# Pairs of branch weights in one fetch, one summed block of squares per norm, and one activation part kept twice, in a hybrid decoder layer

## The chip, the cores and the metric

The kernel runs on one NeuronCore of a Trainium2 chip. The metric is the device time of one execution in microseconds; for a kernel the median of several executions is given. TensorE (PE) multiplies, VectorE (DVE), ScalarE (ACT) and GpSimd (POOL) work on elements, and SyncE (SP) issues most of the DMAs.

## The reference

One decoder layer for a single sequence of 256 tokens, model width 2048, all in float32:

```python
h = rms_norm(x, ln1)
proj = h @ w_in                      # gdn q|k|v, beta, decay, z, moba q|k|v, gate a, gate b
y_a = gated_deltanet(...) @ w_branch_a      # 8 heads of 128, chunks of 64
y_b = moba_attention(...) @ w_branch_b      # 8 heads of 128, 256 tokens are one block: causal attention
merged = sigmoid(gate_a) * y_a + sigmoid(gate_b) * y_b
x = x + merged @ w_out
h = rms_norm(x, ln2)
u = causal_dwconv(h @ w_up, ffn_conv, bias)  # width 3, 2 x 5632 columns
x = x + (silu(u_gate) * u_val) @ w_down
return rms_norm(x, final_norm)
```

`rms_norm(x, w)` is `x * rsqrt(mean(x * x) + 1e-6) * w`.

## The kernel before, in words

**Arithmetic.** Each large product is made of three products of rounded parts. A weight is split into a high part `wh` (its value rounded to the type that PE reads, fp32r) and a low part `wl` (the rest); an activation into `one(k, 0)` and `one(k, 1)` in the same way. `block` multiplies, for each block k of 128 input channels, `wh` by the high part, `wh` by the low part and `wl` by the high part, and adds all of it up in one PSUM tile. The channels of the output lie on the partitions and the 256 tokens on the free axis, so that a product has a 128x128 weight block and 256 moving columns. The norms' factor per token (`R1`, `R2`) is multiplied in after the product (`join`), so that PE needn't wait for it.

**Stages, in the order of the program.** The first gdn blocks, in which the inputs arrive; then gdn and z (three chunks and one, for four pairs of heads), moba q and k (eight chunks) with v (four chunks of another form), gate (16 chunks), the two branch projections, called br (8 times a chunk for branch a and one for branch b), wo (8 chunks), up (44 chunks) and down, with the final norm. A chunk is two output blocks of 128 channels. It has 96 main products where the input has 16 blocks (gdn, z, moba, gate, wo, up), and 48 in br, whose input has 8.

**Weights.** `fetch` lets SP copy a weight block into one of four `wraw` buffers of 128x2048 words. `load_w` then makes the parts in pieces of 1024 columns: ACT casts (`wh`, L121) and DVE subtracts (`wl`, L118). There are two `wh` and two `wl` tiles, which take turns, and one call of `load_w` takes one of each, whatever it puts in. In br a call brings 1024 columns, half a tile, and in the other stages 2048.

**Background.** The short steps of the delta rule and of attention are generators in a list `bg`; each time that the main products' estimated cost passes `EVERY`, `tick` advances them by a step. Their small products stand between main products in PE's queue until the gate stage is some chunks old.

**Where operands lie.** `Parts` holds both parts of an activation in one tile, for k = 0 to 15 the high part and then the low part, 256 words each. After the eighth k there is a gap of 64 words, and `TURN` (0 here) could move a low part into it. Weights start 24 words into their tile (`PLACE`, 8 for v).

**Kicks.** Before a chunk that `KICKS` names (gate 7, wo 1, up 1, 12, 23 and 34) three products with 128 moving columns are issued into a tile that nobody reads.

**Norms.** ACT squares, DVE and POOL add blocks of channels up, and `rstd` sums over the partitions with products by a tile of ones (float32, L99). For the first norm two blocks of 128x256 are left at that point, for the second four, which come as two pairs (`sqa`, and `sq` of the last chunk).

**The end.** For each of two halves of the tokens and four column blocks n, ACT squares the finished sum in PSUM (L836), and for n < 3 DVE multiplies it by the final norm's weights (L839). Then come a reduction (L840), a square root, a reciprocal (L842), and the scaling of the four blocks (L845 for n = 3, L847, L849) with their output DMAs.

The order on each engine is set by the framework's scheduler from its own simulation, and each engine works strictly along its list.

Of the kernel before, what the change touches and what calls it, by code (L numbers as in the profile page):

```python
# [11 lines left out]
F32 = mybir.dt.float32  # L12
# [17 lines left out]
PLACE = {"v": 8}  # L30
TURN = 0
KICKS = {"gate": (7,), "wo": (1,), "up": (1, 12, 23, 34)}
GROUP = 8
ATT_SCALE = 128 ** -0.5
# [49 lines left out]
def layer_kernel(ctx: ExitStack, tc: tile.TileContext, xT, pos, cst, csel, ceye, vec, convw, ffw, bdv,  # L84
# [68 lines left out]
    class Parts:  # L153


        def __init__(self, pool, kt, name, **kw):
            self.size = GROUP * 2 * T + 64
            self.flat = pool.tile([P, kt // GROUP * self.size], F32R, name=name, **kw)

        def at(self, k, a):  # L160
            return k // GROUP * self.size + (2 * (k % GROUP) + a) * T + TURN * (a and k % GROUP == GROUP - 1)

        def one(self, k, a):
            o = self.at(k, a)
            return self.flat[:, o:o + T]

        def two(self, k, a):
            o, step = self.at(k, a), self.at(k + 1, a) - self.at(k, a)
            if o + 2 * step <= self.flat.shape[1]:
                return self.flat[:, o:o + 2 * step].rearrange("p (b t) -> p b t", b=2)[:, :, :T]  # L170
            o -= step - T
            return self.flat[:, o:o + 2 * step].rearrange("p (b t) -> p b t", b=2)[:, :, step - T:]

# [14 lines left out]

    def block(ps, j, w, x, kt, k0=0, k1=None):
        wh, wl = (r3(t, P) for t in w)  # L190
        for k in range(k0, k1 or kt):
            for w_, a in ((wh, 0), (wh, 1), (wl, 0)):
                main_mm(ps[:, j], w_[:, k, :], x.one(k, a), j == k == a == 0 and w_ is wh,
                        k == kt - 1 and w_ is wl)

    def chunk(blocks, x, kt, name, raws=(None, None), piece=1024, steps=((0, 0, None), (1, 0, None)), c=None):
        ps = mmt("ps_" + name)
        ws = {}
        if c in KICKS.get(name, ()):
            ws[0] = load_w(blocks[0], kt * P, raw=raws[0], piece=piece, at=PLACE.get(name, 24))  # L200
            idle = sdt("kick")
            for _ in range(3):
                pe.matmul(idle[:, :P], ws[0][0][:, :P], x.one(0, 0)[:, :P], start=True, stop=True)
        for j, k0, k1 in steps:
            if j not in ws:
                ws[j] = load_w(blocks[j], kt * P, raw=raws[j], piece=piece, at=PLACE.get(name, 24))
            block(ps, j, ws[j], x, kt, k0, k1)
        return ps
# [23 lines left out]
    hp = hst.enter_context(tc.tile_pool(name="hp", bufs=1, side="right"))  # L232
    hc = Parts(hp, KD, "hc", tag="hc")
    front = ExitStack()
# [28 lines left out]
    for i in range(4):  # L263
        scaled(xs[:, 4 * i:4 * i + 4, :], ln1v, 4 * i, hc)
    raws = [fetch(w) for w in (w_gdn[2], w_gdn[3])]
    wbd = g.tile([P, KD, 16], F32, name="wbd")
# [29 lines left out]
    dve.tensor_tensor(sq[0], sq[0], sq[2], op=ALU.add)  # L296
    dve.tensor_tensor(sq[0][:, 0:2], sq[0][:, 0:2], sq[0][:, 2:4], op=ALU.add)


# [5 lines left out]
    mmg(s, [(wb2[:, k, :], hc.one(k, a)) for k in range(KD) for a in range(2)])  # L305
    R1 = rstd([sq[0][:, 0, :], sq[0][:, 1, :]], fk, "R1")
    R1b = both(R1)
# [420 lines left out]
    for c in range(8):  # L728
        bts = [yp.tile([P, 2, T], F32, name="bt", bufs=3) for _ in range(2)]
        join(bts[0], chunk(pair(w_ba, c), yc[0], H, "br"), gts[:, c])  # L730
        ps = chunk(pair(w_bb, c), yc[1], H, "br")
        if c < 7:
# [16 lines left out]
    sqa = b.tile([P, 2, T], F32, name="sqa", bufs=1)  # L749
    h2 = Parts(hp, KD, "h2", tag="hc")  # L750
    for c in range(8):
# [8 lines left out]
        if c == 0:  # L760
            act.activation(sqa, xc, AF.Square)
        else:
            sq = b.tile([P, 2, T], F32, name="sq2")
            act.activation(sq, xc, AF.Square)
            if c < 7:
                pool.tensor_tensor(sqa, sqa, sq, op=ALU.add)
    R2 = rstd([t[:, j, :] for t in (sqa, sq) for j in range(2)], bkeep, "R2")
    R2b = both(R2)
# [31 lines left out]
    def residual(i, n):  # L800
# [5 lines left out]
    wl = {}  # L806
    tail = hp.tile([P, KD // GROUP * (GROUP * 2 * T + 64)], F32R, name="tail", tag="hc")[:, :8192].rearrange(
        "p (t k n) -> p t k n", t=2, k=2)

# [19 lines left out]
    for i in range(2):  # L829
        sm = b.tile([P, 8], F32, name="sm")  # L830
        ots = []
        for n in range(4):
            for k in range(NF - LAST, NF):
                down(i, n, k, stop=(k == NF - 1))
            scr = b.tile([P, 512], F32, name="scr")
            act.activation(scr, pd[i][n], AF.Square, accum_out=sm[:, n:n + 1])  # L836
            ots.append(b.tile([P, 512], F32, name="ot_", bufs=5))
            if n < 3:
                dve.tensor_tensor(ots[n], pd[i][n], fw[:, n * 512:(n + 1) * 512], op=ALU.mult)  # L839
# [3 lines left out]
        for n in range(4):  # L843
            if n == 3:
                dve.scalar_tensor_tensor(ots[n], pd[i][n], sm[:, 6:7], fw[:, n * 512:], op0=ALU.mult, op1=ALU.mult)  # L845
# [71 lines left out]
```

## Time and profile before

| | |
|---|---|
| median of 3 executions | 1497.35 us (1497.07 to 1499.13) |
| the profiled execution | 1498.51 us, its span 1496.7 us |
| mean granted TensorE clock | 0.997 |
| PE busy | 1478.6 us, 11489 products |
| DVE, ACT, POOL busy | 967.8, 720.9, 121.2 us |
| read from HBM | 271.68 MB, 184 GB/s over the span |

The span runs from the first to the last instruction on the core; 1.8 us of the time lie around it. Products are pipelined: one of 256 columns is listed with 276 ns, but the next starts some 113 ns after it. "PE busy" therefore says that PE nearly always has a product under way, and not how fast they follow each other. The chain of waits gives the latter: its pieces join instructions that followed each other, with their count.

### The profile page before, as it was taken

What the parts mean: (1) busy time and instruction counts of PE and PEld (TensorE: products, weight loads), DVE (VectorE), ACT (ScalarE), POOL (GpSimd) and SP (SyncE); (2) the same over time, 40 slices, a digit from 0 to 9 for tenths busy, and PEclk for the clock granted to TensorE, in tenths of its full rate; (3) what the DMA queues carried; (4) which work ended last, traced back from release to release, by engine and by line L of the source; (5) the groups of instructions that cost most, each with busy time, mean ns of one, the idle gap of its engine ahead of it and who ended that gap; (6) DMA issues with size and microseconds to landing.
All of it is one profiled execution on the core that took longest, in us unless ns stands there. A gap on an engine that the chain in (4) does not pass through costs nothing.

```text
span 1496.7 us, 26967 instructions
## 1 busy us (share of the span) xinstructions
PE 1478.6 (99%) x11489; PEld 1418.4 (95%) x11489; DVE 967.8 (65%) x1373; ACT 720.9 (48%) x948; POOL 121.2 (8%) x133
## 2 busy tenths in 40 slices
PE   9999999999999999999999999999999999999998
PEld 8999999998999999999999999999999998888886
DVE  7978786896656545666666666666666665555554
ACT  5655363434474444345455544454554544444444
POOL 0001010141121000110100000000000000000000
PEclk9999999999999999999999999999999999999999
DMA  9545444444436554568555555555555555555552
GB/s 334 182 150 185 152 155 169 150 149 164 145 115 207 191 195 127 183 209 318 191 186 197 196 189 186 193 195 197 197 196 187 189 194 177 189 196 194 197 197 85
DMA packets 45658, 277.23 MB, mean 185 GB/s; under 512 B 5505, under 2 KB 6993, under 8 KB 15457
## 3 DMA queue, kind: packets, MB, share of 16 engines
q1 hardware_dynamic: 43712, 270.98, 52.7%
q0 software_dynamic: 960, 2.36, 0.5%
q10 hardware_dynamic: 864, 2.16, 0.4%
q8 instruction: 90, 1.47, 0.4%
q14 instruction: 32, 0.25, 0.0%
HBM read 271.68 MB, written 3.80 MB: 184 GB/s over the span
## 4 chain that ended last, share of the span: by engine, by line
PE 91%; DVE 4%; DMA 2%; ACT 1%; issue 1%; SPq 0%; DVEq 0%; ACTq 0%
PE ps_up L111 32%; PE pd L99 16%; PE ps_gate L111 11%; PE ps_gdn L111 8%; PE ps_wo L111 5%; PE ps_br L111 5%; PE ps_moba L111 4%; PE ps_v L111 3%; PE ps_z L111 3%; DVE wl L118 2%; DMA wraw<-in_w_gdn 1%; ACT wh L121 1%; DMA x<-in_xT 1%; PE g L99 1%; PE py L558 1%
## 5 line engine op out<-in xcount | busy, mean ns | idle before, releaser
L118 DVE TENSOR_TENSOR wl<-wraw,wh 128x1024 fp32r<-128x1024 f32 (+1 forms) x500 | 607.1, 1248 | 214.6 <-ACT wh L121 214.3
L121 ACT CAST wh<-wraw 128x1024 fp32r<-128x1024 f32 (+1 forms) x500 | 497.7, 1040 | 466.2 <-PE ps_up L111 162.7
L111 PE MATMUL ps_up<-h,wh 128*128 128x256 f32 x2816 | 479.7, 276 | 0.0
L111 PEld LDWEIGHTS ps_up<-h,wh 128*128 128x128 f32 x2816 | 424.2, 188 | 0.1
L111 PE MATMUL ps_up<-h,wl 128*128 128x256 f32 x1408 | 388.6, 276 | 0.0
L111 PEld LDWEIGHTS ps_up<-h,wl 128*128 128x128 f32 x1408 | 264.3, 188 | 0.0
L111 PE MATMUL ps_gate<-hc,wh 128*128 128x256 f32 x1024 | 176.8, 278 | 0.0
L111 PEld LDWEIGHTS ps_gate<-hc,wh 128*128 128x128 f32 x1024 | 154.6, 188 | 0.0
L111 PE MATMUL ps_gate<-hc,wl 128*128 128x256 f32 x512 | 141.9, 277 | 0.4 <-DVE wl L118 0.4
L99 PE MATMUL pd<-wl,ah 128*128 128x512 f32 x336 | 130.8, 389 | 0.0
L99 PE MATMUL pd<-wh,al 128*128 128x512 f32 x336 | 130.8, 389 | 0.0
L111 PE MATMUL ps_gdn<-hc,wh 128*128 128x256 f32 x704 | 126.7, 283 | 0.0
L111 PEld LDWEIGHTS ps_gdn<-hc,wh 128*128 128x128 f32 x704 | 108.9, 191 | 0.9 <-ACT wh L121 0.3
L111 PE MATMUL ps_gdn<-hc,wl 128*128 128x256 f32 x352 | 99.8, 284 | 0.8 <-DVE wl L118 0.8
L111 PEld LDWEIGHTS ps_gate<-hc,wl 128*128 128x128 f32 x512 | 96.2, 188 | 0.6 <-DVE wl L118 0.6
L111 PE MATMUL ps_moba<-hc,wh 128*128 128x256 f32 x512 | 93.1, 283 | 0.0
L99 PE MATMUL pd<-wh,ah 128*128 128x512 f32 x336 | 92.8, 391 | 0.0
L212 DVE TENSOR_TENSOR unf<-ps_up,R 128x512 f32<-128x512 f32 x44 | 30.4, 691 | 90.1 <-PE ps_up L111 90.1
L111 PE MATMUL ps_wo<-mc,wh 128*128 128x256 f32 x512 | 87.3, 276 | 0.0
L111 PEld LDWEIGHTS ps_moba<-hc,wh 128*128 128x128 f32 x512 | 78.6, 189 | 0.2
L111 PEld LDWEIGHTS ps_wo<-mc,wh 128*128 128x128 f32 x512 | 77.2, 188 | 0.0
L99 PEld LDWEIGHTS pd<-wh,al 128*128 128x128 f32 x336 | 63.1, 188 | 13.3
(426 smaller groups left out, 1966.5 us busy)
## 6 DMA issues: line engine op xcount, KB each, us to landing
wraw<-in_w_up SPq DMA_DIRECT2D x88, 1024.0 KB, 4.9
wraw<-in_w_dn SPq DMA_DIRECT2D x44, 1024.0 KB, 4.8
wraw<-in_w_gate SPq DMA_DIRECT2D x32, 1024.0 KB, 4.9
wraw<-in_w_gdn SPq DMA_DIRECT2D x30, 1024.0 KB, 5.0
wraw<-in_w_moba SPq DMA_DIRECT2D x16, 1024.0 KB, 4.9
wraw<-in_w_o SPq DMA_DIRECT2D x16, 1024.0 KB, 4.9
wraw<-in_w_mv SPq DMA_DIRECT2D x8, 1024.0 KB, 5.0
wraw<-in_w_ba SPq DMA_DIRECT2D x16, 512.0 KB, 3.5
```

Source lines behind the costliest of these rows:

```text
L99: pe.matmul(ps, a, b, start=(start and i == 0), stop=(stop and i == n - 1), **kw)
L111: pe.matmul(ps, a, b, start=start, stop=stop, skip_group_check=True)
L118: return (eng or dve).tensor_tensor(lo, src, hi.bitcast(F32), op=ALU.subtract)
L121: act.copy(hi, src)
L212: dve.tensor_tensor(dst, ps, r, op=ALU.mult)
L558: pe.matmul(py[:, p], ats[p], Tm[:, p], start=True, stop=True)
```

## The change

- **Branch weights.** On the host, two neighbouring blocks of `w_branch_a` and of `w_branch_b` are laid side by side (`by_pair`). A chunk in br calls `load_w` once, with one DMA of 2048 columns in place of two of 1024, and both halves lie in one `wh` and one `wl` tile.
- **Norms.** DVE adds the two last blocks of squares (for the second norm the last chunk's pair too), and `rstd` has one product in place of two, and of four.
- **A second copy.** The tile of `hc` and `h2` has room behind the 16 blocks. For the first norm's `hc` ACT copies the low part of k = 11 there, 48 words behind the blocks' end; gdn, z and moba read this copy in place of the first, while gate, v and the beta and decay products read the first. (All other moving blocks start a multiple of 64 words apart, before as after.) The gap of 64 words after the eighth k is gone.
- **Kicks.** Gate 7, up 1 and up 23 are left.
- **The end.** In the second half of the tokens DVE multiplies the block n = 3 by the norm's weights before the reduction, as for the other n, and then scales it from SBUF.

```diff
-TURN = 0
-KICKS = {"gate": (7,), "wo": (1,), "up": (1, 12, 23, 34)}
-GROUP = 8
+TURN = 48
+TURNED = (11,)
+KICKS = {"gate": (7,), "up": (1, 23)}
...
-        def __init__(self, pool, kt, name, **kw):
-            self.size = GROUP * 2 * T + 64
-            self.flat = pool.tile([P, kt // GROUP * self.size], F32R, name=name, **kw)
-
-        def at(self, k, a):
-            return k // GROUP * self.size + (2 * (k % GROUP) + a) * T + TURN * (a and k % GROUP == GROUP - 1)
-
-        def one(self, k, a):
-            o = self.at(k, a)
-            return self.flat[:, o:o + T]
+        def __init__(self, pool, kt, name, turned=0, **kw):
+            self.kt = kt
+            self.flat = pool.tile([P, kt * 2 * T + turned * (64 + len(TURNED) * T)], F32R, name=name, **kw)
+            self.all = self.flat[:, :kt * 2 * T].rearrange("p (k s t) -> p k s t", s=2, t=T)
+
+        def one(self, k, a, turn=False):
+            if turn and a and k in TURNED:
+                o = self.kt * 2 * T + TURN + TURNED.index(k) * T
+                return self.flat[:, o:o + T]
+            return self.all[:, k, a, :]
...
-                main_mm(ps[:, j], w_[:, k, :], x.one(k, a), j == k == a == 0 and w_ is wh,
+                main_mm(ps[:, j], w_[:, k, :], x.one(k, a, turn), j == k == a == 0 and w_ is wh,
                         k == kt - 1 and w_ is wl)
...
         ps = mmt("ps_" + name)
         ws = {}
+        if kt == H:
+            w = load_w(blocks, 2 * kt * P, at=24)
+            ws = {j: [t[:, j * kt * P:(j + 1) * kt * P] for t in w] for j in range(2)}
...
-            block(ps, j, ws[j], x, kt, k0, k1)
+            block(ps, j, ws[j], x, kt, k0, k1, name in ("gdn", "z", "moba"))
...
+    for k in TURNED:
+        act.copy(hc.one(k, 1, True), hc.one(k, 1).bitcast(F32))
...
     dve.tensor_tensor(sq[0][:, 0:2], sq[0][:, 0:2], sq[0][:, 2:4], op=ALU.add)
+    dve.tensor_tensor(sq[0][:, 0], sq[0][:, 0], sq[0][:, 1], op=ALU.add)
...
-    R1 = rstd([sq[0][:, 0, :], sq[0][:, 1, :]], fk, "R1")
+    R1 = rstd([sq[0][:, 0, :]], fk, "R1")
...
-        join(bts[0], chunk(pair(w_ba, c), yc[0], H, "br"), gts[:, c])
-        ps = chunk(pair(w_bb, c), yc[1], H, "br")
+        join(bts[0], chunk(w_ba[c], yc[0], H, "br"), gts[:, c])
+        ps = chunk(w_bb[c], yc[1], H, "br")
...
-            if c < 7:
-                pool.tensor_tensor(sqa, sqa, sq, op=ALU.add)
-    R2 = rstd([t[:, j, :] for t in (sqa, sq) for j in range(2)], bkeep, "R2")
+            (pool if c < 7 else dve).tensor_tensor(sqa, sqa, sq, op=ALU.add)
+    dve.tensor_tensor(sqa[:, 0], sqa[:, 0], sqa[:, 1], op=ALU.add)
+    R2 = rstd([sqa[:, 0, :]], bkeep, "R2")
...
-            if n < 3:
+            if n < 3 or i == 1:
                 dve.tensor_tensor(ots[n], pd[i][n], fw[:, n * 512:(n + 1) * 512], op=ALU.mult)
...
-            if n == 3:
+            if n == 3 and i == 0:
                 dve.scalar_tensor_tensor(ots[n], pd[i][n], sm[:, 6:7], fw[:, n * 512:], op0=ALU.mult, op1=ALU.mult)
...
+    def by_pair(w):
+        return w.reshape(-1, 2, P, w.shape[2]).transpose(0, 2, 1, 3).reshape(w.shape[0] // 2, P, -1)
...
-        "w_ba": blocks(np.asarray(w_branch_a)[0]),
-        "w_bb": blocks(np.asarray(w_branch_b)[0]),
+        "w_ba": by_pair(blocks(np.asarray(w_branch_a)[0])),
+        "w_bb": by_pair(blocks(np.asarray(w_branch_b)[0])),
```

Apart from line numbers (L840, L841, L843, L846, L848 and L850 of the new end are L839, L840, L842, L845, L847 and L849 before), the engines' lists differ in few places. The three that follow are those on which the prediction rests.

DVE's list in br before, for the first two times round: `bt` is the branch's result times its gate, `wl` the low part of weights, `mc` the low part of the merged activation.

```order
L212 TENSOR_TENSOR bt<-ps_br,gts 128x512
L118 TENSOR_TENSOR wl<-wraw,wh 128x1024 x2
L212 TENSOR_TENSOR bt<-ps_br,gts 128x512
L118 TENSOR_TENSOR wl<-wraw,wh 128x1024
L118 TENSOR_TENSOR mc<-gts,mc 128x2x256
L118 TENSOR_TENSOR wl<-wraw,wh 128x1024
```

The same place of the change:

```order
L211 TENSOR_TENSOR bt<-ps_br,gts 128x512
L118 TENSOR_TENSOR wl<-wraw,wh 128x1024 x2
L211 TENSOR_TENSOR bt<-ps_br,gts 128x512
L118 TENSOR_TENSOR wl<-wraw,wh 128x1024 x2
L118 TENSOR_TENSOR mc<-gts,mc 128x2x256
```

The subtraction for `mc` stood between the two weight pieces after every second join, and now stands behind both.

DVE's list around the second norm of the change (R is `R2`, `h` the split activation of up, `unf` the first joined product of up); before, the two rows with `sqa` weren't there, and the reciprocal stood ahead of the two `wl`:

```order
L216 SCALAR_TENSOR_TENSOR h_7341<-x_7339,vc,h_7341 128x256 x2
L767 TENSOR_TENSOR sqa<-sqa,sq_8317 128x512
L768 TENSOR_TENSOR sqa<-sqa 128x256
L118 TENSOR_TENSOR wl<-wraw,wh 128x1024 x2
L224 RECIPROCAL R_8323<-R_8323 128x256
L211 TENSOR_TENSOR unf<-ps_up,R_8323 128x512
```

On PE the norm's products stood in two pairs, one ahead of up's first product and one 28 rows (42 products) later; now there is a single product, 46 rows (69 products) into up's first chunk.

DVE's list at the end of the change, with what each row waits for (`pd` are the finished sums in PSUM, `fw` the final norm's weights):

```order
L840 TENSOR_TENSOR ot__15499<-pd_2_13858,fw 128x512 [waits DMAHW4_49,Activation_49]
L840 TENSOR_TENSOR ot__15515<-pd_3_13859,fw 128x512 [waits DMAHW5_49,DVE_49,Activation_49]
L841 TENSOR_REDUCE sm<-sm 128x1
L843 RECIPROCAL sm<-sm 128x1 [waits Activation_49]
L850 TENSOR_SCALAR ot__15467<-ot__15467,sm 128x512 [waits DVE_49]
L850 TENSOR_SCALAR ot__15499<-ot__15499,sm 128x512
L850 TENSOR_SCALAR ot__15515<-ot__15515,sm 128x512
```

Its second row is new there, ahead of the reduction, and the last one reads the prepared block; before, the list had L839 three times, the reduction, the reciprocal, L849 twice, and one product of three factors (L845) that read PSUM.

More of the change, by code (lines that the diff above doesn't have):

```diff
@@ L153, in layer_kernel @@
     class Parts:
-        def __init__(self, pool, kt, name, **kw):
-            self.size = GROUP * 2 * T + 64
-            self.flat = pool.tile([P, kt // GROUP * self.size], F32R, name=name, **kw)
-        def at(self, k, a):
-            return k // GROUP * self.size + (2 * (k % GROUP) + a) * T + TURN * (a and k % GROUP == GROUP - 1)
-        def one(self, k, a):
-            o = self.at(k, a)
-            return self.flat[:, o:o + T]
-        def two(self, k, a):
[L168 to L172, printed above, removed]
+        def __init__(self, pool, kt, name, turned=0, **kw):
[7 more added lines that the diff above has]
+            return self.all[:, k, a, :]
+        def two(self, k, a):
+            return self.all[:, k:k + 2, a, :]
     def psum_pools(mm, sd):
@@ L187, in sdt, with block @@
         return pst[1].tile([P, 512], F32, name=name, tag="sd")
-    def block(ps, j, w, x, kt, k0=0, k1=None):
+    def block(ps, j, w, x, kt, k0=0, k1=None, turn=False):
         wh, wl = (r3(t, P) for t in w)
@@ L232, in layer_kernel @@
     hp = hst.enter_context(tc.tile_pool(name="hp", bufs=1, side="right"))
-    hc = Parts(hp, KD, "hc", tag="hc")
+    hc = Parts(hp, KD, "hc", 1, tag="hc")
     front = ExitStack()
@@ L749, in layer_kernel @@
     sqa = b.tile([P, 2, T], F32, name="sqa", bufs=1)
-    h2 = Parts(hp, KD, "h2", tag="hc")
+    h2 = Parts(hp, KD, "h2", 1, tag="hc")
     for c in range(8):
@@ L806, in layer_kernel @@
     wl = {}
-    tail = hp.tile([P, KD // GROUP * (GROUP * 2 * T + 64)], F32R, name="tail", tag="hc")[:, :8192].rearrange(
-        "p (t k n) -> p t k n", t=2, k=2)
+    tail = Parts(hp, KD, "tail", 1, tag="hc").flat[:, :8192].rearrange("p (t k n) -> p t k n", t=2, k=2)
     def down(i, n, k, stop=False):
```

## The prediction

> **What bounds the kernel now.** I read the page's busy times first, then the chain of waits by engine.
>
> ```profile
> PE 1478.6 (99%) x11489; PEld 1418.4 (95%) x11489; DVE 967.8 (65%) x1373; ACT 720.9 (48%) x948; POOL 121.2 (8%) x133
> PE 91%; DVE 4%; DMA 2%; ACT 1%; issue 1%; SPq 0%; DVEq 0%; ACTq 0%
> ```
>
> PE sets the time nearly everywhere, so that a product taken out of its list, or a closer sequence of products, shortens the whole. The question is how fast products follow each other in each stage. The chain's pieces in order of time (start, us, engine, name, line, count) tell it:
>
> ```profile
> 60.38 16.49 PE ps_gdn L111 x140
> ...
> 225.78 2.12 PE ps_moba L111 x18
> ...
> 282.67 4.77 PE ps_moba L111 x40
> ...
> 486.14 97.99 PE ps_gate L111 x864
> 584.13 10.78 PE ps_br L111 x95
> ...
> 606.67 1.06 ACT wh L121
> ...
> 607.76 2.19 DVE wl L118
> ...
> 609.99 8.13 PE ps_br L111 x69
> ...
> 676.08 3.97 PE ps_wo L111 x35
> ...
> 1017.11 119.75 PE ps_up L111 x1056
> ```
>
> In up a product takes 119.75 / 1056 = 113.4 ns, in gate 113.4, but in this long piece of gdn 117.8, with the same shapes. (A short piece reads longer, since its first and last steps belong to the break.) In br the chain leaves PE in each round for a cast and a subtraction (3.3 us), which happens nowhere else so regularly. The views of the single tiles give each form's duration as minimum/median/maximum:
>
> ```profile
> L111 PE MATMUL ps_gdn<-hc,wh x704: 276/281/582, 20.6 to 211.8; 128*128 128x256 f32 x176
> L111 PE MATMUL ps_z<-hc,wh x256: 276/281/364, 48.0 to 225.4; 128*128 128x256 f32 x128
> L111 PE MATMUL ps_moba<-hc,wh x512: 276/281/369, 225.6 to 394.7; 128*128 128x256 f32 x171
> L111 PE MATMUL ps_up<-h,wh x2816: 276/276/470, 764.6 to 1245.6; 128*128 128x256 f32 x188
> ```
>
> The listed duration follows the pace: 281 at 117.8, 276 at 113.4. So there are two steady paces, and the slower one is the commoner in gdn, z and moba, where background products break into the main ones.
>
> **Br: fetching in pairs.** What PE waited for in the time of br (us in total, times, longest), one round of br on ACT and DVE, and one of wo:
>
> ```profile
> PE ps_br L111 <- DVE wl L118: 2.1, 7, 0.3
> ...
> 594.93 1.05 ACT L121 CAST wh<-wraw 128x1024 fp32r<-128x1024 f32 x1 [1.67 <-PE ps_br L111]
> 597.14 0.62 ACT L121 CAST mc<-gts 128x512 fp32r<-128x512 f32 x1 [1.16 <-POOL gts L734]
> 596.01 2.17 DVE L118 TENSOR_TENSOR wl<-wraw,wh 128x1024 fp32r<-128x1024 f32 x1 [0.28 <-ACT wh L121]
> 598.11 0.68 DVE L118 TENSOR_TENSOR mc<-gts,mc 128x512 fp32r<-128x512 f32 x1
> 753.18 2.00 ACT L121 CAST wh<-wraw 128x1024 fp32r<-128x1024 f32 x2 [3.40 <-PE ps_wo L111]
> 754.26 2.36 DVE L118 TENSOR_TENSOR wl<-wraw,wh 128x1024 fp32r<-128x1024 f32 x2 [0.28 <-ACT wh L121]
> ```
>
> A weight tile comes free when PE has finished the block in it: 24 products, 24 x 0.1134 = 2.72 us. Cast (1.05) and subtraction (1.2, half of 2.36) with the waits between take about 2.6 us, so anything beside them is late; here the subtraction that overlaps the merge on POOL takes 2.17. After the change a tile holds 48 products, 5.44 us, for two casts and two subtractions, which the last two rows, from wo, show: from 753.18 to 756.62 is 3.4 us. A join runs beside the casts, and `mc` (0.68) now stands behind both pieces, which makes 4.2 us: over a microsecond is left in each round. wo's casts and subtractions have this rhythm already. The 32 DMAs become 16 on the same queue, and the four `wraw` buffers reach twice as far ahead. I cost the stage at the free pace: 768 x 0.1134 = 87.1 us, against 676.08 - 584.13 = 91.95. Gain 4.9 us. Bounds: half of it, if the merge still held ACT up in each round (2.4), and 4.9.
>
> **The short products.** On PE's timeline (start, us, then the number of records; a float32 product leaves two):
>
> ```profile
> 763.86 0.28 PE L111 MATMUL ps_wo<-mc,wl 128*128 128x256 f32 x1
> 763.98 1.02 PE L99 MATMUL R<-sqa,ones 128*128 128x256 f32 x4
> ...
> 765.07 0.28 PE L111 MATMUL ps_up<-h,wl 128*128 128x256 f32 x1
> ...
> 896.53 0.28 PE L111 MATMUL ps_up<-h,wl 128*128 128x256 f32 x1
> 896.64 0.44 PE L203 MATMUL kick<-h,wh 128*128 128x128 f32 x3
> ...
> 897.21 0.28 PE L111 MATMUL ps_up<-h,wl 128*128 128x256 f32 x1
> ```
>
> From 763.86 to 765.07 there would be three steps of 113 ns, 0.34 us; it took 1.21. A pair of norm products thus costs 0.87 us, a single one 0.43. One falls away at the first norm, three at the second: 1.73 us. A kick costs 897.21 - 896.53 - 0.34 = 0.34 us, and three fall away: 1.0 us. Together 2.75 us, all of it on PE. The new additions on DVE cost nothing if they end before PE comes to the product. At the second norm:
>
> ```profile
> 767.41 0.88 DVE L217 SCALAR_TENSOR_TENSOR h<-x,vc,h 128x256 fp32r<-128x256 f32 x2
> 771.18 1.75 DVE L225 RECIPROCAL R<-R 128x256 f32<-128x256 f32 x1 [2.90 <-ACT R L224]
> 776.81 0.69 DVE L212 TENSOR_TENSOR unf<-ps_up,R 128x512 f32<-128x512 f32 x1 [1.67 <-PE ps_up L111]
> ```
>
> `h` ends at 768.3; two additions (0.7 for 512 columns, as `unf` shows, and by estimate 0.4 for half as many) end at 769.4. The one product now stands 69 products into up, at about 764.0 + 7.8 = 771.8, and waits for nothing; if PE came there first, it would wait for 1.1 us at most. The reciprocal then ends near 775.5, ahead of the join at 776; late, it would delay a join, for which PE has two more PSUM tiles. The copy of k = 11 is one cast on ACT, under the 0.62 us of `mc` at twice the size, while the first weights are still under way; without that cover it would cost as much.
>
> **The second copy.** It moves one of 48 products onto an address 48 words off. The trace has no such product in these stages, but it shows that the address can matter: the down products of the last two k read their weights from `tail`, elsewhere within 64 words than the `wh` before (by the kernels' tile addresses), and are slower.
>
> ```profile
> L99 PE MATMUL pd<-tail,ah x32: 389/394/399, 1474.4 to 1488.8; 128*128 128x512 f32 x32
> L99 PE MATMUL pd<-wh,ah x336: 389/389/476, 1246.2 to 1487.1; 128*128 128x512 f32 x168
> ```
>
> My reading: the pace is a phase between weight loads and moving reads; background products set it anew, and a product with another phase in each pass may do so too. There are 1056 + 384 + 768 = 2208 main products in gdn, z and moba. By the medians at least half are slow, at most nearly all but the first 192: I take 70%, 1546 x 4.4 ns = 6.8 us. That is the most that can be gained; if instead all became slow, the rest, 662 x 4.4 = 2.9 us, would be lost. The turned product comes once in 48, while the chain's moba pieces have some 18 to 40 products between background ones, so that about half of the slow products come before it. Value 3.1 us, range -2.9 to 6.8.
>
> The Trainium skill ("TensorE: Matmul & The Clock Gate", section "Back-to-back issue gap") gives a warm gap of N / 2.4 + 2.5 ns, 109 ns for 256 columns, and names no operand address; by it this edit would be worth nothing. The trace disagrees in having two gaps, 113.4 and 117.8, so I don't set it at nothing, but keep it as a rival.
>
> **The end.**
>
> ```profile
> 1488.13 0.69 DVE L839 TENSOR_TENSOR ot__15575<-pd,fw 128x512 f32<-128x512 f32 x1 [0.58 <-ACT scr L836]
> 1490.21 0.16 DVE L840 TENSOR_REDUCE sm<-sm 128x1 f32<-128x4 f32 x1 [1.40 <-ACT scr L836]
> 1491.33 0.48 DVE L849 TENSOR_SCALAR ot__15575<-ot__15575,sm 128x512 f32<-128x512 f32 x1
> 1491.73 0.74 DVE L845 SCALAR_TENSOR_TENSOR ot__15591<-pd,sm,fw 128x512 f32<-128x512 f32 x1
> ```
>
> DVE's multiplication waits for ACT's square of the same block, like the reduction. The added one therefore starts at 1490.21, and the reduction and all behind it come some 0.61 us later; the last scaling gets shorter by 0.74 - 0.48 = 0.26. Loss 0.35 us.
>
> **Sum.** -4.9 - 2.75 - 3.1 + 0.35 = -10.4 us. The profiled execution's 1498.51 becomes 1488.1. It stands 1.16 above the median of the runs, 1497.35, so I forecast 1486.9.
>
> **Rivals.** *The copy does nothing*: gdn, z and moba keep a median of 281. For it: nothing in this trace shows a single main product changing the pace. Against: every break by background products can. -7.3 us, 1490.0. *The copy frees all of it*: the pace stays fast over breaks once it is. -14.1 us, 1483.2. Against it: pieces of 18 to 40 products leave no room for that. *The half-speed stretch moves.* By windows (length, PE busy and its count, granted clock, DMA share, GB/s):
>
> ```profile
> 76.60:80.20 3.60, 3.60 (x24) 0.99 0.81 291
> 80.20:87.00 6.80, 6.80 (x30) 0.50 0.01 2
> ```
>
> After a stretch with only 24 short products PE is granted half its clock for 6.8 us, which costs up to 3.4. The new start shifts PE by about a microsecond here; without the drop the time is 1483.5, with a second one 1490.3. (The Trainium skill, same page, section "The HAM clock gate", has free-running windows of 3.4 us decide this; the 6.8 us are two of them.) *Up falls into the slow pace*, the one that ends on the other side: up has 4224 products, two of its four kicks go, and so does wo's. From kick 1 on, 43 x 96 = 4128 x 4.4 = 18.2 us would be lost: 1505.1. It decides from 10.4 / 0.0044 = 2360 slow products on, more than the 22 chunks between the kicks left. Against it: nothing breaks into up, and its median before is 276 throughout, with pieces of 1056 products at one pace.
>
> **Chances.** Forecast (copy worth 1.5 to 5 us, 1485.0 to 1488.5) 46%; copy worth nothing or a little less (to 1492) 24%; copy worth all 18%; half-speed stretch moved 7%; up slow 5%, in three fifths of it slower than before. Range 1481.5 to 1491.5: it takes in the first four but for their ends. About 0.2%, 3 us, is what can be told from no change. Faster 0.94, same 0.03, slower 0.03.
>
> **What would show it.** br from first to last product in 87 us, without a wait of PE for `wl`; the median of moba at 276, or its chain pieces nearer 113 ns a product; one `R` product of two records per norm; the reduction at the end 0.6 us after ACT's square. I am wrong if br still leaves PE each round, if gdn, z and moba are slower than before, or if up's pieces leave 113.4 ns.

## The result, and the profile after

The changed kernel takes 1487.39 us (median of five executions, 1485.81 to 1490.7), the kernel before, run beside it, 1497.07 (1493.93 to 1499.13). The ratio is 0.994, with a 95% interval of 0.9928 to 0.9952, so 7 to 11 us less. The profiled execution of the change took 1485.81 us (span 1484.0) and stands 1.58 below its median, while that of before (1498.51) stood above its own. The two traces therefore differ by 12.7 us, of which some 3 belong to the choice of these two executions. Below it is shown where they come from.

Busy times of the changed kernel, from the page:

```profile
PE 1467.9 (99%) x11472; PEld 1409.7 (95%) x11472; DVE 968.6 (65%) x1377; ACT 720.1 (49%) x949; POOL 121.9 (8%) x133
```

PE is still the engine that sets the time. The pieces of the changed kernel's chain of waits (start, us, engine, name, line, count):

```profile
60.53 16.09 PE ps_gdn L111 x140
...
578.68 87.04 PE ps_br L111 x768
...
665.72 87.04 PE ps_wo L111 x768
...
752.76 7.82 PE ps_up L111 x69
...
761.01 3.18 PE ps_up L111 x27
...
764.47 239.43 PE ps_up L111 x2112
```

br is now one piece of 768 products at 87.04 / 768 = 113.3 ns, without a cast or a subtraction in the chain, and so is wo. In gdn the piece of 140 products fell from 16.49 to 16.09 us. In up, 27 products took 3.18 us, 117.8 ns each, between the norm's product and the first kick; the 2112 behind the kick ran at 113.4.

The stages, measured on PE's timeline from the first product of one to the first of the next (the start up to z's first product; z with the gdn chunks after it; the end from the last product to the end of the span), in us; the differences are taken before rounding:

| | to z | z, gdn | moba, v | gate | br | wo | up | down | end | span |
|---|---|---|---|---|---|---|---|---|---|---|
| before | 48.0 | 177.6 | 169.3 | 189.0 | 91.95 | 88.73 | 481.20 | 243.2 | 7.69 | 1496.7 |
| after | 47.9 | 172.9 | 169.1 | 188.7 | 87.04 | 87.04 | 479.98 | 243.2 | 8.30 | 1484.0 |
| difference | -0.1 | -4.7 | -0.3 | -0.3 | -4.91 | -1.69 | -1.22 | 0.0 | +0.61 | -12.7 |

The pace of the main products in gdn, z and moba, as minimum/median/maximum of the listed duration, in the changed kernel:

```profile
L111 PE MATMUL ps_gdn<-hc,wh x704: 276/277/467, 20.7 to 207.1; 128*128 128x256 f32 x176
L111 PE MATMUL ps_z<-hc,wh x256: 275/281/365, 47.9 to 220.5; 128*128 128x256 f32 x128
L111 PE MATMUL ps_moba<-hc,wh x512: 276/281/369, 220.8 to 389.6; 128*128 128x256 f32 x171
```

Only gdn's median moved, from 281 to 277; moba's, for which the prediction named 276 as a sign, stayed at 281. If a product counts as slow when the next one starts 116 to 120 ns after it, 1469 of the 2208 products of the three stages were slow before and 908 are after.

The column of z and gdn holds more than this pace. By windows of PE (length, PE busy and its count, granted clock, DMA share, GB/s) of the changed kernel, at the place where the prediction quoted a half-speed stretch:

```profile
76.60:80.20 3.60, 3.60 (x24) 1.00 0.81 291
80.20:87.00 6.80, 6.80 (x56) 1.00 0.15 22
```

The light stretch of 24 products is there as before, and the clock stays at 1.00: 56 products are listed where there were 30.

At the second norm, on PE's timeline of the changed kernel (start, us, records):

```profile
760.30 0.28 PE L111 MATMUL ps_up<-h,wl 128*128 128x256 f32 x1
760.42 0.59 PE L99 MATMUL R<-sqa,ones 128*128 128x256 f32 x2
...
763.20 0.28 PE L111 MATMUL ps_up<-h,wl 128*128 128x256 f32 x1
...
763.91 0.28 PE L111 MATMUL ps_up<-h,wl 128*128 128x256 f32 x1
764.02 0.45 PE L202 MATMUL kick<-h,wh 128*128 128x128 f32 x3
...
764.95 0.28 PE L111 MATMUL ps_up<-h,wl 128*128 128x256 f32 x1
...
765.63 0.28 PE L111 MATMUL ps_up<-h,wl 128*128 128x256 f32 x1
```

One norm product of two records is left, and PE waits for nothing there. Ahead of the kick two steps of three products take 0.71 us, behind it 0.68. At the end, on the timelines of DVE, ACT and ACT's queue of the changed kernel:

```profile
1476.22 0.60 ACT L837 ACTIVATE scr<-pd 128x512 f32<-128x512 f32 x1 [1.40 <-PE pd L99]
1476.94 0.69 DVE L840 TENSOR_TENSOR ot__15515<-pd,fw 128x512 f32<-128x512 f32 x1 [1.40 <-ACT scr L837]
1477.55 0.14 DVE L841 TENSOR_REDUCE sm<-sm 128x1 f32<-128x4 f32 x1
1479.05 0.48 DVE L850 TENSOR_SCALAR ot__15515<-ot__15515,sm 128x512 f32<-128x512 f32 x1
1479.56 0.34 ACTq L851 DMA_DIRECT2D out<-ot__15515  x1
```

The added multiplication waits for ACT's square, and the reduction starts 0.61 us after it, as the prediction had it. The DMA of the last block, before and then after (KB, us from issue to landing):

```profile
out<-ot__15591 ACTq DMA_DIRECT2D x1, 256.0 KB, 3.0
...
out<-ot__15515 ACTq DMA_DIRECT2D x1, 256.0 KB, 3.3
```

### The profile page after: what moved, and what is told of

It reads as the page before. It is cut to its first block, busy times and chain, and to the rows that moved or that the text cites. A ratio compares the mean times of both kernels' runs of the same rounds, so it can differ in the third digit from the quotient of the medians.

```text
span 1484.0 us, 26882 instructions
## 1 busy us (share of the span) xinstructions
PE 1467.9 (99%) x11472; PEld 1409.7 (95%) x11472; DVE 968.6 (65%) x1377; ACT 720.1 (49%) x949; POOL 121.9 (8%) x133
## 3 DMA queue, kind: packets, MB, share of 16 engines
q0 software_dynamic: 960, 2.36, 0.5%
## 4 chain that ended last, share of the span: by engine, by line
PE 91%; DVE 4%; DMA 2%; issue 1%; ACT 1%; SPq 0%; DVEq 0%; POOLq 0%; ACTq 0%
PE ps_up L111 32%; PE pd L99 16%; PE ps_gate L111 11%; PE ps_gdn L111 8%; PE ps_wo L111 6%; PE ps_br L111 6%; PE ps_moba L111 3%; PE ps_z L111 3%; PE ps_v L111 2%; DVE wl L118 1%; DMA wraw<-in_w_gdn 1%; ACT wh L121 1%; PE py L560 1%; PE g L99 0%; PE pu L566 0%
## 5 line engine op out<-in xcount | busy, mean ns | idle before, releaser
L121 ACT CAST ah<-acts 128x256 fp32r<-128x256 f32 x44 | 17.9, 407 | 119.2 <-PE pd L99 118.3
```

The source lines that it names most:

```text
L121: act.copy(hi, src)
```

## Experiments

Each kernel is the changed one with the edit shown. Kernels that ran on one chip share the executions of the kernel before there, so that ratios are compared and not medians. The stages, as above:

| | z, gdn | moba, v | gate | br | wo | up | end | ratio to before (95% interval) |
|---|---|---|---|---|---|---|---|---|
| change | 172.9 | 169.1 | 188.7 | 87.04 | 87.04 | 479.98 | 8.30 | 0.994 (0.9928 to 0.9952) |
| E1 single fetches | 173.0 | 169.3 | 190.6 | 91.67 | 87.04 | 479.98 | 8.28 | 0.9974 (0.9961 to 0.9986) |
| E2 one DMA, two tiles | 172.9 | 168.9 | 190.6 | 91.95 | 87.04 | 479.98 | 8.33 | 0.9963 (0.9948 to 0.9977) |
| E3 copy unread | 174.3 | 169.4 | 190.5 | 87.04 | 87.04 | 479.98 | 8.30 | 0.9951 (0.9936 to 0.9966) |
| E4 copy not moved | 177.6 | 169.6 | 189.1 | 87.04 | 87.04 | 479.98 | 8.29 | 0.9956 (0.9943 to 0.997) |
| E5 two parts moved | 172.5 | 169.0 | 189.6 | 87.04 | 87.04 | 479.98 | 8.29 | 0.9943 (0.9928 to 0.9957) |
| E6 no kick in up | 173.0 | 169.0 | 190.5 | 87.04 | 87.04 | 497.62 | 8.30 | 1.005 (1.003 to 1.007) |
| E7 old end, kick in wo | 172.6 | 169.0 | 189.0 | 87.04 | 87.39 | 479.98 | 7.69 | 0.9929 (0.9915 to 0.9943) |
| E8 later transposes | 173.0 | 171.7 | 185.1 | 87.04 | 87.04 | 479.63 | 7.69 | 0.9929 (0.9913 to 0.9945) |
| E9 old end, one kick less | 172.6 | 169.0 | 192.0 | 87.04 | 87.04 | 479.63 | 7.69 | 0.993 (0.9917 to 0.9942) |
| E10 the change again | 173.0 | 169.2 | 189.1 | 87.04 | 87.04 | 479.98 | 8.30 | 0.9935 (0.9921 to 0.9948) |
| E11 E8 again | 172.6 | 173.0 | 185.1 | 87.04 | 87.04 | 479.63 | 7.69 | 0.9929 (0.9916 to 0.9943) |

### E1 and E2: what in br was worth 4.9 us

My theory was that a weight tile of 48 products gives casts and subtractions their room. The rival is the transfers: half as many, each twice as large. E1 fetches single blocks again, into half-filled tiles. E2 keeps the paired DMA, and lets each half have a tile of its own.

```diff
 E1
-        if kt == H:
-            w = load_w(blocks, 2 * kt * P, at=24)
-            ws = {j: [t[:, j * kt * P:(j + 1) * kt * P] for t in w] for j in range(2)}
...
-        join(bts[0], chunk(w_ba[c], yc[0], H, "br"), gts[:, c])
+        join(bts[0], chunk(pair(w_ba, c), yc[0], H, "br"), gts[:, c])
...
-        "w_ba": by_pair(blocks(np.asarray(w_branch_a)[0])),
+        "w_ba": blocks(np.asarray(w_branch_a)[0]),
 E2
-            w = load_w(blocks, 2 * kt * P, at=24)
-            ws = {j: [t[:, j * kt * P:(j + 1) * kt * P] for t in w] for j in range(2)}
+            raw = fetch(blocks)
+            raws = [raw[:, j * kt * P:(j + 1) * kt * P] for j in range(2)]
+            blocks = [None, None]
```

> Only the branch weights are undone: two DMAs of 1024 columns per chunk, each half in its own wh and wl tile, as before the change. Theory (a tile that holds 24 products comes back too late for a cast and a subtraction plus whatever stands beside them): from br's first product to wo's first 91.9 us, with seven waits of PE for wl, against 87.1 with pairs; median 4.8 us above the changed kernel's 1487.4, so 1492.2. Rival (the stage's gain came from PE's own pace, by what lies ahead of it in the program): br stays at 87 us and the median at 1487.4.

> One DMA of 2048 columns per chunk, as in the change, but each half is split into a wh and a wl tile of its own, as before. Theory (the tile, not the transfer, decides): br takes 91.9 us as with single fetches, median 1492.2. Rival (half as many and larger DMAs, and deeper prefetch, made the gain): br takes 87.1 us, median 1487.4.

What PE waited for in br of E1 (us in total, times, longest), one of these waits on its timeline, and its DMAs (count, KB each, median us from issue to landing):

```profile
PE ps_br L111 <- DVE wl L118: 2.2, 7, 0.3
...
594.70 0.39 PE L111 MATMUL ps_br<-yca,wh 128*128 128x256 f32 x2
595.37 0.39 PE L111 MATMUL ps_br<-yca,wl 128*128 128x256 f32 x1 [0.29 <-DVE wl L118]
595.60 0.40 PE L111 MATMUL ps_br<-yca,wh 128*128 128x256 f32 x2
...
wraw<-in_w_ba SPq DMA_DIRECT2D x16, 512.0 KB, 3.5
```

The waits and the DMAs of E2:

```profile
PE ps_br L111 <- DVE wl L118: 2.1, 7, 0.3
...
wraw<-in_w_ba SPq DMA_DIRECT2D x8, 1024.0 KB, 4.9
```

And the pair of subtractions beside the merge, in br of the changed kernel:

```profile
590.56 3.32 DVE L118 TENSOR_TENSOR wl<-wraw,wh 128x1024 fp32r<-128x1024 f32 x2 [0.28 <-ACT wh L121]
```

With the paired DMA of the change (8 of 1024 KB for each branch), E2 has all seven waits of before and its 91.95 us, and E1 has them with the single ones. Size and number of the DMAs don't matter here, and the tile that a weight half lies in does: this is shown. One thing comes along with the tile and isn't separated from it: in E1 and E2 DVE's list has the `mc` subtraction between the two weight pieces again, as before. The merge still slows the subtraction beside it (3.32 us for the pair, against 2.36 in wo); with 48 products in a tile PE doesn't wait for it. A reading to keep: the waits view lists 0.3 us for each, but the seven cost 91.67 - 87.04 = 4.63 us, 0.66 each. The timeline says why in part: from 594.70 to 595.60 three steps took 0.90 us in place of 0.34. A pipelined product is listed as busy for 0.28 after its start, though its successor could have started after 0.11.

### E3 and E4: what the copy does, and whether it must be moved

E3 makes the copy and reads the first everywhere. E4 reads the copy, which now starts a multiple of 64 words from the others.

```diff
 E3
-            block(ps, j, ws[j], x, kt, k0, k1, name in ("gdn", "z", "moba"))
+            block(ps, j, ws[j], x, kt, k0, k1)
 E4
-TURN = 48
+TURN = 0
```

> The copy of k = 11 is still made, but gdn, z and moba read the first place. Theory (the moved product pulls PE out of the slower pace): the median product of gdn, z and moba is listed with 281 ns again, slow products cost some 2 us more from 37 us to the start of gate, median 1489.5. Rival (the gain in these stages came only from the norm's product and the half-speed stretch): medians of the changed kernel stay, time 1487.4.

> The copy of k = 11 is read by gdn, z and moba as in the change, but it begins a multiple of 64 words from the other blocks (48 words taken off its place). Theory (the place within 64 words decides): as without the copy: the product with k = 11 is followed by the next after 113 or 118 ns like all others, medians 281 ns in gdn, z and moba, time about 1490. Rival (any other place in the tile, or reading another block than the neighbours', does it): as the changed kernel, medians 276 to 278, 1487.4.

Main products of gdn in E3, as minimum/median/maximum:

```profile
L111 PE MATMUL ps_gdn<-hc,wh x704: 276/281/468, 20.9 to 208.5; 128*128 128x256 f32 x176
```

And in E4, with the piece of its chain that took 16.09 us in the change:

```profile
L111 PE MATMUL ps_gdn<-hc,wh x704: 276/281/582, 20.7 to 211.9; 128*128 128x256 f32 x176
...
60.50 16.49 PE ps_gdn L111 x140
```

Both are back at the medians of before, E4 although it reads another place. So the offset within 64 words decides and not the copy. What follows from it is seen on PE's timeline. The changed kernel, at a pass over k = 11; the `wh` row at 86.42 holds two products, and the second reads the copy:

```profile
83.48 0.28 PE L111 MATMUL ps_gdn<-hc,wl 128*128 128x256 f32 x1
...
86.31 0.28 PE L111 MATMUL ps_gdn<-hc,wl 128*128 128x256 f32 x1
86.42 0.40 PE L111 MATMUL ps_gdn<-hc,wh 128*128 128x256 f32 x2
...
87.02 0.28 PE L111 MATMUL ps_gdn<-hc,wl 128*128 128x256 f32 x1
...
87.37 0.28 PE L111 MATMUL ps_gdn<-hc,wl 128*128 128x256 f32 x1
...
91.79 0.28 PE L111 MATMUL ps_gdn<-hc,wl 128*128 128x256 f32 x1
```

The same stretch of the program in E4, up to the next break:

```profile
87.93 0.28 PE L111 MATMUL ps_gdn<-hc,wl 128*128 128x256 f32 x1
...
97.11 0.28 PE L111 MATMUL ps_gdn<-hc,wl 128*128 128x256 f32 x1
```

From 83.48 to 87.02 lie ten steps of three products, 0.354 us each (118 ns a product); from 87.37 to 91.79 thirteen, 0.340 each (113.3). Nothing but main products stands between. In E4 the 26 steps to the break all take 0.353. Over all passes over k = 11 with no background product near: in the change 14 of 18 that come in at 118 ns leave at 113.3, and 14 of 14 that come in at 113.3 keep it; before, 22 of 22 that come in at 118 ns keep that, and in E4 25 of 25. In E10, the change run again, it is 15 of 19. That the moved product frees the pace is thus shown. It has a price: in a sequence at 113.3 ns the steps around it take 122, 118, 117 and 116 ns, about 20 ns a pass.

What it is worth: E3's gate starts at 391.6 us, the change's at 389.8, that is 1.8 (the seven traces with one code up to gate, those of the change, E1, E2, E6, E7, E9 and E10, have it at 389.1 to 390.5, so 1.1 to 2.5); the ratios 0.9951 against 0.994 and 0.9935 say 1.6 to 2.4 us, with intervals that overlap. E4's 177.6 in z and gdn needs the windows (length, PE, its weight loads, DVE, ACT and POOL, then clock, DMA share, GB/s):

```profile
80.20:87.00 6.80, 6.80 (x29) 6.16 (x29) 4.28 (x12) 5.23 (x5) 0.60 (x1) 0.50 0.01 2
```

E4's profiled execution has the half-speed stretch of before at the same place, E3's doesn't. At the same pace of products it costs 177.6 - 174.3 = 3.3 us. The difference of 4.7 us in z and gdn between before and after is therefore 3.3 of clock and 1.4 of pace.

### E5: a second moved part

If one moved part frees the pace after k = 11, a second one, at k = 3, should free it sooner. E5 moves the first copies themselves in both blocks, without a second copy, so that gate, v and the decay products read them too.

```diff
-TURNED = (11,)
+TURNED = (3, 11)
...
-            if turn and a and k in TURNED:
+            if self.moved:
+                o = (2 * k + a) * T + 64 * sum(m < k for m in self.moved) + TURN * (a and k in self.moved)
...
-    hc = Parts(hp, KD, "hc", 1, tag="hc")
+    hc = Parts(hp, KD, "hc", 1, TURNED, tag="hc")
...
-    for k in TURNED:
-        act.copy(hc.one(k, 1, True), hc.one(k, 1).bitcast(F32))
```

> In the first norm's activation the low parts of k = 3 and k = 11 lie 48 words off in place (no copy; 64 words of room behind each), so that all stages that read it, gate and v too, have two moved products in 48. Theory (each moved product frees PE from the slow pace, and costs some 20 ns where PE is fast): slow products in gdn, z and moba fall below those of the change, which loses 4.3 us there, by 1 to 1.5 us, while the moved ones cost 0.9 us more; in gate they cost 2 x 32 x 0.02 = 1.3 us less what the freed first chunks bring (0.5). Time 0.5 to 1 us above the change. Rival (one moved product in 48 is too rare, and its own price nothing): 1.5 us below the change.

Main products of gdn in E5:

```profile
L111 PE MATMUL ps_gdn<-hc,wh x704: 276/276/468, 21.0 to 207.0; 128*128 128x256 f32 x176
```

The median is 276, and z and gdn gain 0.4 us. Gate, most of which runs without a break, is 0.5 to 0.9 us longer than in the change and E10: there both places pay their price and gain little. The sum is the change's, 0.9943 against 0.994; from z to br the traces have 531.1 us, and 530.6 and 531.2 in the change and E10, so that neither the 0.5 to 1 us more nor the 1.5 us less that were named beforehand shows. The number of places is a trade between breaks and price, and one place, read only where there are breaks, is about as good as two.

### E6: the kicks that are left

The rival of the other side was up in the slow pace. E6 takes the last two kicks out of up.

```diff
-KICKS = {"gate": (7,), "up": (1, 23)}
+KICKS = {"gate": (7,)}
```

> Both kicks in up are left out, gate's is kept. In the changed kernel the norm's single product in up leaves PE at 0.35 us for three products, and the kick at chunk 1 brings back 0.34. Theory (the pace holds until something breaks in): up stays slow from the norm's product to its end, 43.3 chunks x 96 x 4.4 ns = 18.3 us more, less 0.7 for two kicks: median 1505. Rival (PE comes back by itself within some products, the kicks are no use): pieces of up at 113.4 ns a product, median 1486.7.

The chain of E6 in up, and the tile's durations:

```profile
754.23 7.82 PE ps_up L111 x69
...
762.48 489.37 PE ps_up L111 x4155
...
L111 PE MATMUL ps_up<-h,wh x2816: 276/281/468, 754.1 to 1251.4; 128*128 128x256 f32 x188
```

The single norm product leaves PE at 489.37 / 4155 = 117.8 ns, and it stays there for all of up: 17.6 us more than with the kicks, and a kernel slower than before. So the rival was real, and one kick of 0.34 us holds it off: in the change it stands 27 products behind the norm's product. The second kick left does nothing that shows; E8, E9 and E11 do without it and have up in 479.63 us, 0.35 less.

### E7 to E11: the end, and a wait before gate

E7 takes the old end and puts wo's kick back. E9 takes the old end and drops up's kick 23. E8 and E11, one kernel run on two chips, are E9 with attention's transposes three steps of the background later, since PE waits there for the softmax. E10 is the change, run beside E9 and E11.

```diff
 E7, E8, E9, E11
-            if n < 3 or i == 1:
+            if n < 3:
...
-            if n == 3 and i == 0:
+            if n == 3:
 E7
-KICKS = {"gate": (7,), "up": (1, 23)}
+KICKS = {"gate": (7,), "wo": (1,), "up": (1, 23)}
 E8, E9, E11
-KICKS = {"gate": (7,), "up": (1, 23)}
+KICKS = {"gate": (7,), "up": (1,)}
 E8, E11
-        yield from wait(2)
+        yield from wait(5)
```

> Two undone parts in stages that the trace tells apart: the last block is multiplied by the norm's weights behind the reduction, as before, and the kick at wo 1 is back. Theory for the end (the multiplication that waits for ACT's square delays the reduction by 0.61 and saves 0.26): from PE's last product to the end of the span 0.35 us less than in the change (8.30). Rival: the change's end is the shorter one. For wo: with the kick 87.04 + 0.34 = 87.4 us from its first product to up's if the wait of 0.5 us for the late residual in the kernel before was no matter of the kick; 87.9 or more if the kick brings that wait.

> The change with the old end, without the kick at up 23, and with moba's transposes three background steps later. In the profiles PE waits some 2 us for the last heads' softmax at the start of gate, and is granted half its clock for 3.4 us right after it in four of six. Theory (the light stretch there is what loses the clock): gate shorter by 2 us where the clock fell and no half-speed stretch at 400 us; end -0.35, kick -0.34; median 1484.5. Rival (the stretch falls with the phase of the clock's own windows, whatever PE does there): only -0.7 and the wait itself, median 1486.

> The change with the old end and without the kick at up 23, moba's transposes where the change has them. From PE's last product to the end of the span 7.69 us (8.30 in the change), up 0.35 shorter: 0.95 us below the change. If the half-speed stretch at 400 us belongs to the wait for the last softmax, some of its executions lose 1.9 us there; if not, they spread as those with the later transposes do.

> The changed kernel itself, on the chip of the other two, to compare with: about 1487.4 by its first five executions; 0.95 us above the kernel with the old end.

> The kernel with the old end, without the kick at up 23, and with moba's transposes three background steps later, again, beside the two others. Theory (PE no longer waits 2 us for the last softmax): about 1 us below the kernel with the old end alone, by the profiles' moba (2.7 us longer) and gate (3.6 us shorter than in the change where the clock held); 1484.5.

The end takes 7.69 us in all four runs with the old one and in before, and 8.28 to 8.33 in all with the new: 0.61 us lost. Wo with its kick is 87.39, without 87.04; the chain of E7 shows the place, 0.28 us between two pieces:

```profile
665.57 10.88 PE ps_wo L111 x96
...
676.73 76.22 PE ps_wo L111 x672
```

The wait that E8 was to remove stands in the waits of the change:

```profile
PE pT L662 <- DVE s__3819 L656: 2.0, 1, 2.0
```

E8's waits no longer have that row. Gate gets 3.6 us shorter than the change's, and moba with v 2.7 us longer (E11: 3.6 and 4.0). The sum of the two is 357.7 in the change, 358.1 in E7, 358.3 in E10, 356.8 in E8 and 358.1 in E11. Attention's work was moved from one stage into the other, and the wait came back in another place: PE waits for `wl` in v, 0.7 us in E8 and 1.9 in E11, which it doesn't in the change, and for 0.9 in place of 0.4 us in gate.

E9's 192.0 in gate holds a half-speed stretch, for about 1.5 us, and for as much again slow products, 502 of them where E1, E3 and E6 have about 170. The stretch by windows (PE alone, then clock, DMA share, GB/s), from E3, which has one too, and then the same place in the change:

```profile
398.20:401.70 3.50, 1.51 (x13) 1.00 0.38 108
401.80:405.20 3.40, 3.40 (x16) 0.50 0.42 178
...
394.70:398.20 3.50, 2.97 (x26) 1.00 0.00 0
398.20:401.70 3.50, 2.03 (x16) 1.00 0.87 300
```

In E3, after 3.5 us in which PE was busy for 1.51, it has half its clock for 3.4 us. The change has the same wait, but there it falls into two windows, and the clock stays. E1, E2, E3, E6 and E9 have the half-speed stretch in their profiles, with gate at 190.5 to 192.0. The change, E4, E5, E7 and E10, with 188.7 to 189.6, don't have it. E8 and E11 have none. What goes with it is in the traces. The times at which the clock changes lie whole multiples of 3.413 us apart in all thirteen (22 and 2 of them, 75.09 and 6.83 us, in the kernel before, 116 and 1, 395.95 and 3.41 us, in E3). Counted on this grid, the window ahead of the drop held 1.42 to 1.50 us of listed work in the five that have it, while the emptiest window at this place held 1.55 us in E10 and 1.8 to 2.4 in the kernel before, the change, E4, E5 and E7, which don't. By these traces it is where the wait falls on the grid that makes the difference, though no run shifted it on purpose; and in E8 and E11 PE is busy all through these windows. Their executions, though, still lie between 1483.5 and 1489.8 us, and what the slow ones among them lose isn't traced.

The medians don't tell these versions apart: beside the change (1486.35 in E10) E9 took 1486.4, where 0.95 us less was expected, and E11 1485.71; E7 (1485.42) and E8 (1484.3) have no change beside them. E10 itself is 1.0 us below what was expected of it. All four ratios are 0.9929 or 0.993, and their intervals overlap with the change's. The traces alone tell the stages apart: 0.61 us at the end, and 0.35 where a kick is less. By them the best version I can name is the change with the old end and without up's kick 23.

## Why the prediction came out

The forecast was 1486.9 us, and 1487.39 was measured. Its terms, against the traces:

- **Br, -4.9.** Measured -4.91, by the mechanism given; E1 and E2 rule out the transfers. The room was less than worked out: with 3.32 us for the two subtractions beside the merge, and not 2.36, about 0.4 us are left by the prediction's own sum in place of over a microsecond.
- **Short products, -2.75.** At the second norm and in wo and up the sum holds: wo without its kick (0.34, E7) and without the pair of norm products (0.87), and up -1.22 for two kicks and one norm product. No run undoes the norms alone; this is read from the traces. At the first norm, 0.43 was predicted and 0.1 at most came: the products there do follow 0.43 us sooner, but PE then waits for z's weights, 1.1 us (before 0.8). From the first decay product to the end of this wait 22.06 us pass before and after (32.63 to 54.69, and 32.78 to 54.84). I had named no cover there. A first use of new weights was waiting behind the saved product.
- **Wo, not in the sum.** 1.69 = 0.34 + 0.87 + 0.48. The 0.48 is a wait of PE for `wl` in wo's time before (0.4 in the waits), gone in the change. E7 has wo's kick and not the wait, so the kick wasn't its cause. E1 has neither, with single fetches. The chain of the kernel before shows what that `wl` stood behind, the addition of the residual, whose transfer was late:

```profile
680.98 10.37 DMA x<-in_xT
...
692.08 1.23 DVE wl L118
```

The transfer took 10.37 us and landed 15.4 us after wo's first product; in the twelve other traces it took 7.6 to 8.9 and landed at 13.9 or earlier. Since E1 fetches as the kernel before and hasn't got it, it may belong to that one execution; why it was late isn't settled.
- **Second copy, -3.1.** The mechanism held, that a single product read from another place sets the pace anew; that this is a phase between loads and reads, no run shows. The size did not hold: 1.8 us by E3. I had set the slow products at 70%, 1546, and half of them freed. 1469 were slow, and 38% were freed (908 are left). The price of the moved product itself, some 20 ns in each fast pass, was not in the sum, and neither were the 4 of 18 slow passes that stay slow.
- **The end, +0.35.** The step on the reduction was right, 0.61 us. The step that failed is "the last scaling gets shorter by 0.26". It does: the output's DMA is issued only 0.33 us later relative to ACT's square (3.34 against 3.01 us). But from its issue to the end of the span another 0.28 are lost. The four outputs land one behind the other, 0.6 to 0.7 us apart in both traces, and the first of them is issued 0.60 us later with the reduction; the last one's earlier issue is spent in its transfer, 3.3 us in place of 3.0. So nothing of the 0.26 came back. Measured +0.61.
- **The half-speed stretch, a rival with 7%.** The profiled execution before has it and that of the change hasn't: 3.3 us of their 12.7. Without it they differ by 9.4, the medians by 9.7 and the fastest executions by 8.1. As the price of the edit it isn't one: executions of one kernel lie up to 6 us apart (before 1493.9 to 1499.1, E4 1487.8 to 1494.0), E4 has the stretch with nearly all of the change in it, and profiles with and without a stretch differ by 1.5 to 1.9 us in gate and by 3.3 at this place. The prediction took the stretch of the one trace for a property of the kernel.
- **Up slow, 5%.** The price was right, 17.6 us against 18.2 in the prediction. Its reason against, that nothing breaks into up, was wrong: the norm's product does, and PE ran slow behind it for 27 products. What held it off was the kick at chunk 1, which the prediction counted but didn't credit.

The sum of 10.4 came near the measured 9.7 partly by luck, since misses of both signs met: the copy, the first norm and the end brought 1.3, 0.3 and 0.3 us less, wo 0.5 and up 0.1 more, which gives -9.1. The remaining 0.3, against the 9.4 of the traces without the half-speed stretch, lies in gate (189.0 and 188.7), is less than the 0.4 by which the change and E10, one kernel, differ there, and isn't traced.

The Trainium skill's gap of 109 ns ("TensorE: Matmul & The Clock Gate", "Back-to-back issue gap") was the rival "the copy does nothing". The section gives it for a product by itself and says that in a stream of loads and products both set the spacing, so it was no fair forecast for these stages. The measured gaps are 113.3 and 117.8 ns, and E3 and E4 show that an operand's address can choose between them, which the formula has no term for. Its "The HAM clock gate" says that windows of 3.4 us decide the clock. The stretches here were 3.4 and 6.8 us long, on one grid, in agreement. But it has the clock fall after an idle window, while at 400 us a window with 1.42 to 1.50 us of work was enough, and the stretch at 80 us followed 3.6 us in which PE is listed as busy throughout, if with only 24 products.

## What to carry to other kernels

When parts of a double-buffered operand are made on the way, count the consumer's time per buffer and not per byte: a buffer only half filled has only half of its time to be refilled, whatever the transfers do, and the waits view shows less than half of what that costs a pipelined engine. A pace of products read from pieces of the chain, rather than from busy time, tells whether a stage runs in the faster or the slower of two states. Where a break by other products leaves the slower one, a few short products behind it are a cheap insurance; here the one behind the norm's product in up was worth 17.6 us, and those that were left out, in wo and later in up, nothing that shows. Two profiles differ by whatever the clock did in those two executions; subtract that from their difference before crediting an edit.

## What the runs showed of the hardware

- Products of the same shape, 128x128 by 256 columns with new weights each, run at one of two steady paces, 113.3 or 117.8 ns, and keep it: 4155 products in a row at the slow one in E6, 2112 at the fast one in the change.
- What changes the pace: a break by products of other forms can leave it either way; three products of 128 columns brought up back to the fast one (118 to 113.4 ns in the change; without them 117.8 to the end of up in E6); in gdn, z and moba one product that reads its moving operand 48 words off the 64-word raster of the others did so in 14 of 18 cases. An operand elsewhere on that raster never did (0 of 25 in E4). What happens inside PE isn't in these traces and stays open.
- The clock fell to 0.50 for 6.8 us after 3.6 us with only 24 products, and for 3.4 us after 3.5 us with 1.51 us of work. Its changes lie on a grid of 3.413 us; at 400 us it fell after the five windows of this grid with 1.42 to 1.50 us of work, and not after those with 1.55 or more. It cost 1.5 to 1.9 us in gate (E3's 190.5 against 189.1 in E10 and 188.7 in the change) and 3.3 at 80 us (z and gdn in E4 against E3). That executions of one kernel differ by it isn't seen in two traces of one kernel, but their mean granted clock follows their time (E9: 0.997 at 1487.5 us, 0.999 at 1485.2).
